# Weight sums staged in three tiles where rotation and decay tables lay, and GpSimd's order of sums and transfers written down

## Chip, cores and metric

One core of a Trainium2 chip. The metric is the device time of one execution in microseconds (us), the median of three runs. A profile of one further execution says what each engine did: TensorE (PE, its weight loads PEld), VectorE (DVE), ScalarE (ACT), GpSimd (POOL) and SyncE (SP), which here only issues transfers.

## What is computed

One inference step of a decoder layer over 1,088 tokens: a prompt of 1,024, and 8 sequences of 8 new tokens. All arrays are float32. Cut to what matters here:

```
h    = rmsnorm(x); proj = h @ w_in            # 1024 -> 4096 + 8 gates
ret  = retention(rotary(q), rotary(k), v)     # 4 heads of 128, in chunks of 128 tokens, decay tables
ml   = mlstm(q, k, v, gates)                  # 4 heads of 128, in chunks of 128 tokens
x    = x + rmsnorm(concat(ret, ml) @ w_out)
up   = rmsnorm(x) @ w_up                      # 1024 -> 2 * 2816 (gate and value)
act  = gelu(conv3(up)[gate]) * conv3(up)[value]
y    = x + rmsnorm(act @ w_down)
```

## The kernel before

A matrix product in float32 precision is made of three products of rounded halves: each operand is split into a high half (ACT, line 145) and a rest (DVE, line 147), and PE does high by high, high by rest and rest by high (lines 159 to 161 for the first two projections, 964 to 966 for the up-projection). The 1,088 tokens are four blocks of 272 columns.

Stages, in order of time: the retention heads with their projections (`mix_head(hd, False)`), the mLSTM heads (`mix_head(hd, True)`), the last gate projections with `mix_split`, the output projection (`out_proj`), the up-projection with convolution and gelu (one tile of 128 gate and 128 value columns per step, 22 steps, j = 0 to 21), and the down-projection.

The up-projection of tiles 2 to 21 uses a Strassen scheme of seven products in place of eight. It needs four sums of the four blocks A11, A12, A22 and A21 of each weight tile. They do not depend on the tokens, so they are made long before: `weight_sums` (line 689) runs on GpSimd while PE works on the mLSTM heads. For each of 40 parts (20 tiles, two halves of 256 columns each) it

- fetches the four blocks from `in_wu` in two transfers of 256 KB (line 698, issued on GpSimd's queue) into a tile of 128 x 1024,
- makes four sums in place, each 128 x 256 (line 710), the first three in a chain, where each reads the one before,
- stores the tile with one transfer of 512 KB to a DRAM scratch `sd` (line 711, GpSimd's queue too).

The up-projection later loads the sums from `sd` (line 904, two transfers of 256 KB for each pair of sums).

There are two tiles for the parts. They lie where the rotation tables `rot0` and `rot1` were, so the first fetch waits until the last retention head has rotated its keys (lines 440 and 441). The fetch of a part writes a tile whose earlier store has to land first. The retention's other tables (decay masks, `C_RM`, `C_RMS`; factors `C_ZE`, `C_XI`, `C_XI2`) and the identity are one tile `cst`; their last reader is the last retention head's `finish` (lines 593 and 596).

The order of instructions on an engine is set by a scheduler from estimated times, unless the program fixes it with `tc.issue_after(x)`: what is issued in that context comes behind x. All instructions of one engine run in that order, and one that waits holds up those behind it.

All tiles of the mixing stages lie in pools that are closed by `mixctx.close()` (line 745); the pool `fp`, which has the accumulators `oacc` of the output projection (line 791), tiles for its weights and the loads `xr` (line 816), is laid over their memory. A first write to such a tile waits for everything that still used the memory under it, the sums' tiles and their stores included. The output projection takes its weight tiles m = 0 to 7 through two staging tiles `st_out` (SP, line 133), and its first weight tiles are not in `fp`.

Of the kernel before, what the change touches and what calls it, by code (L numbers as in the profile page):

```python
# [10 lines left out]
F32 = mybir.dt.float32  # L11
# [3 lines left out]
ALU = mybir.AluOpType  # L15

P = 128
D = 1024
# [4 lines left out]
TS = NB * LS  # L23
T = LP + TS
# [12 lines left out]
HB = 2 * Q  # L37
# [7 lines left out]

C_ID, C_RM, C_RMS = 0, 128, 128 + 512
C_ZE, C_XI, C_XI2, C_BLK = C_RMS + 256, C_RMS + 264, C_RMS + 300, C_RMS + 336
C_N = C_BLK + 8
X_NEG, X_NEGS, X_SEL = 0, 128, 192
# [43 lines left out]
def hybrid_layer_kernel(ctx: ExitStack, tc: tile.TileContext, a: dict, o: dict):  # L93
    nc = tc.nc
# [125 lines left out]
    mp = mpool("mp", bufs=1)  # L220
    cst = mp.tile([P, C_N], F32, name="cst")
    rb = mp.tile([P, T], F32, name="rb")
# [9 lines left out]
    xs = [flat("x", b, k=KT) for b in range(4)]  # L232
    rot = [mp.tile([P, T], F32, tag=f"rot{i}", name=f"rot{i}") for i in range(2)]
    nc.sync.dma_start(vec, a["vec"])
    first = (2 * NH, 2 * NH + 1)
    staged = [stage_w(a["wi"][first[0]], f"in{first[0]}")]
    for b in range(4):
# [5 lines left out]
        if b == 1:  # L243
            for i in range(2):
                nc.sync.dma_start(rot[i], a["rot"][:, i * T:(i + 1) * T])
    nc.sync.dma_start(cst, a["cst"])
    nts = []
# [229 lines left out]
    def mix_head(hd, ml):  # L477
# [38 lines left out]
        def front(cs):  # L516
# [8 lines left out]
            if ml:  # L525
                nc.vector.tensor_tensor(kz[:n, :L], px[:n, 0, :L, :],
                                        cols[:n, c0:c0 + L, NH + hd].unsqueeze(2).broadcast_to([n, L, P]), ALU.mult)
            else:
                zc = C_ZE + hd + (0 if c0 < 8 else NH)
                nc.vector.tensor_scalar(kz[:n, :L], px[:n, 0, :L, :], cst[:n, zc:zc + 1], None, ALU.mult)  # L530
            vt = vts[0]
# [26 lines left out]
            else:  # L558
                m = cst[:, C_RM + hd * P:C_RM + (hd + 1) * P] if c0 < 8 else \
                    cst[:TS, C_RMS + hd * TS:C_RMS + (hd + 1) * TS]  # L560
                mk = m.unsqueeze(1).broadcast_to([n, L, n])
# [14 lines left out]
        def finish(on, mv, c0, L, name):  # L576
# [13 lines left out]
            else:  # L590
                xs_ = lambda t: cst[:n, t + 9 * hd + c0:t + 9 * hd + c0 + L]
                rd = xs_(C_XI)
# [96 lines left out]
    def weight_sums():  # L689
# [4 lines left out]

        def fetch(j, c):
            g = mp.tile([P, T], F32, tag=f"rot{c}", name=f"sg{j}_{c}")[:, :D]
            for q in range(2):
                nc.gpsimd.dma_start(g[:, q * 512:(q + 1) * 512].rearrange("p (b n) -> p b n", b=2),  # L698
                                    a["wu"][j, q].rearrange("p (b n) -> p b n", b=2)[:, :, cols(c)])
            held.append(g.rearrange("p (b n) -> p b n", b=4))  # L700

        fetch(*parts[0])
        for i, (j, c) in enumerate(parts):
            if i + 1 < len(parts):
                fetch(*parts[i + 1])
            g = held.pop(0)
            a11, a12, a22, a21 = (g[:, i, :] for i in range(4))
            for o_, x, y, op in ((a21, a11, a21, ALU.subtract), (a22, a22, a21, ALU.subtract),
                                 (a11, a22, a11, ALU.add), (a12, a12, a22, ALU.subtract)):
                nc.gpsimd.tensor_tensor(o_, x, y, op)  # L710
            nc.gpsimd.dma_start(sd[j][:, :, cols(c)], g)
            if c:
                yield
# [166 lines left out]
    def weight_prep(j):  # L880
# [19 lines left out]
        yield ws  # L900
        for i, names in ((1, ("S2", "S1")), (2, ("S4", "S3"))):
            st = wp.tile([P, 2 * HB], F32, tag="wst", name=f"st_up{j}_{i}")[:, :D]
            for c, name in enumerate(names):
                nc.sync.dma_start(st[:, c * D // 2:(c + 1) * D // 2], sd[j][:, ("S1", "S4", "S2", "S3").index(name), :])
            parts(i, st, *names)
            yield
# [431 lines left out]
```

## Time and profile before

| what | value |
|---|---|
| median of three runs | 1419.82 us (1418.65 to 1426.08) |
| the profiled execution: its own time | 1415.93 us |
| its span, from the first to the last instruction | 1414.1 us |
| granted TensorE clock, mean | 0.984 of full speed |
| busy: PE, PEld | 1346.1 us, 1320.2 us |
| busy: DVE, ACT, POOL | 1026.0 us, 587.9 us, 474.1 us |
| DMA: mean rate | 136 GB/s |

The profile page gives busy time by engine, then the span in 40 slices (35.4 us each), then groups of instructions by line. In such a group `out<-in` are names of the program, `x160` is a count, then come the busy time, the mean time of one in ns, and the idle time of the engine just before them with what ended it. "A <- B: total, times, longest" says that A waited for B. The chain that ended last is followed back from the last instruction. In a timeline a row is: start, duration, engine, line, operation, and in brackets the engine's idle time before it and what ended that.

### The profile page before, as it was taken

The numbers are of one execution on the slowest core, as the hardware profiler recorded it, in microseconds if no ns is written. First come the engines' busy times: TensorE is split into PE (matmuls) and PEld (weight loads), VectorE is DVE, ScalarE is ACT, GpSimd is POOL, SyncE is SP. The second block draws the span as 40 slices with busy tenths as digits, with TensorE's granted clock in tenths as the row PEclk, the third lists the DMA queues.
The fourth block names the chain that finished last, engine by engine and source line by source line (L and its number), as shares of the span: only waits on it lengthen the run. The fifth ranks groups of instructions, "written<-read, shape, count | busy, mean of one in ns | idle before, by whom it ended". The sixth has DMA issues, their size and how long they took to land.

```text
span 1414.1 us, 26967 instructions
## 1 busy us (share of the span) xinstructions
PE 1346.1 (95%) x10545; PEld 1320.2 (93%) x10545; DVE 1026.0 (73%) x2023; ACT 587.9 (42%) x1102; POOL 474.1 (34%) x605
## 2 busy tenths in 40 slices
PE   7999899999999998299999999999999999999995
PEld 7899899999999988299999999999999999999995
DVE  7845974566465477156889987877877888996677
ACT  6423542313223234144556444433433445454563
POOL 5200000366556667400243422122222126782000
PEclk9999999999999999699999999999999999999998
DMA  6112111366666655532314444344444359543363
GB/s 235 60 46 70 51 53 60 120 198 168 177 173 164 198 149 167 191 124 64 124 47 140 148 156 128 116 138 145 138 138 130 114 166 321 187 123 94 94 214 127
DMA packets 98494, 192.80 MB, mean 136 GB/s; under 512 B 16832, under 2 KB 41536, under 8 KB 97856
## 3 DMA queue, kind: packets, MB, share of 16 engines
q1 hardware_dynamic: 86208, 149.14, 32.8%
q0 software_dynamic: 12160, 41.95, 10.2%
q8 instruction: 83, 1.36, 0.4%
q14 instruction: 43, 0.35, 0.1%
HBM read 134.58 MB, written 56.47 MB: 135 GB/s over the span
## 4 chain that ended last, share of the span: by engine, by line
PE 65%; DMA 15%; POOL 8%; DVE 7%; issue 3%; ACT 2%; DVEq 0%; SPq 0%; POOLq 0%; ACTq 0%
DMA sg<-in_wu 8%; POOL sg L710 6%; DMA sd<-sg 6%; PE up_S L966 6%; PE up_S L965 6%; PE up_S L964 6%; PE dn L1161 4%; PE dn L1163 4%; PE dn L1162 4%; PE up_A L965 4%; PE up_A L964 4%; PE up_A L966 4%; PE in L161 4%; PE in L159 4%; PE in L160 4%
## 5 line engine op out<-in xcount | busy, mean ns | idle before, releaser
L159 PE MATMUL in<-hh,wh_in 128*128 128x272 f32 x1024 | 302.7, 296 | 12.2 <-ACT hh L199 6.8
L161 PE MATMUL in<-hh,wl_in 128*128 128x272 f32 x1024 | 300.4, 294 | 1.9 <-DVE wl_in L147 1.9
L160 PE MATMUL in<-hl,wh_in 128*128 128x272 f32 x1024 | 299.1, 292 | 1.2 <-DVE hl L200 1.2
L159 PEld LDWEIGHTS in<-hh,wh_in 128*128 128x128 f32 x1024 | 194.6, 190 | 14.9 <-ACT hh L199 6.8
L160 PEld LDWEIGHTS in<-hl,wh_in 128*128 128x128 f32 x1024 | 194.6, 190 | 3.9 <-issue 2.1
L161 PEld LDWEIGHTS in<-hh,wl_in 128*128 128x128 f32 x1024 | 193.9, 190 | 3.3 <-DVE wl_in L147 2.3
L145 ACT ACTIVATE wh_up<-st_up 128x1024 fp32r<-128x1024 f32 x84 | 80.5, 958 | 160.2 <-PE up_S L965 96.4
L710 POOL TENSOR_TENSOR sg<-sg 128x256 f32<-128x256 f32 x160 | 125.9, 815 | 58.0 <-DMA sg<-in_wu 55.6
L147 DVE TENSOR_TENSOR wl_up<-st_up,wh_up 128x1024 fp32r<-128x1024 f32 x84 | 96.8, 1153 | 7.9 <-ACT wh_up L145 7.8
L1090 DVE TENSOR_TENSOR rb<-rb 128x544 fp32r<-128x544 f32 x78 | 73.7, 950 | 34.6 <-ACT rb L1089 34.4
L938 DVE TENSOR_TENSOR Uv<-Uv,up_S 128x272 f32<-128x272 f32 (+1 forms) x200 | 66.6, 376 | 44.2 <-PE up_S L966 44.2
L994 POOL TENSOR_TENSOR act<-act 128x544 f32<-128x544 f32 x44 | 71.5, 1624 | 80.4 <-DMA bd<-act 57.4
L698 POOL DMA_DIRECT2D sg<-in_wu x80 | 57.2, 721 | 80.4 <-DMA sd<-sg 47.2
L1110 POOL TENSOR_TENSOR wd<-wd 128x512 f32<-128x512 f32 x44 | 75.7, 1747 | 23.6 <-DMA wd<-in_wd 12.5
L1089 ACT ACTIVATE rb<-rb 128x544 fp32r<-128x544 f32 x78 | 50.6, 651 | 75.4 <-DMA rb<-bd 63.1
L979 DVE SCALAR_TENSOR_TENSOR c<-Uv,vec,c 128x1024 f32<-128x1024 f32 (+1 forms) x88 | 70.5, 804 | 9.2 <-ACT c L977 9.2
L979 DVE SCALAR_TENSOR_TENSOR c<-Ug,vec,c 128x1024 f32<-128x1024 f32 x88 | 68.6, 818 | 1.9 <-ACT c L977 1.9
L159 PE MATMUL out<-mh,wh_out 128*128 128x272 f32 x128 | 39.2, 306 | 27.4 <-ACT wh_out L145 24.1
L977 ACT ACTIVATE c<-Ug,vec 128x1024 f32<-128x1024 f32 (+1 forms) x44 | 34.7, 835 | 54.9 <-DVE Ug L942 48.8
L145 ACT ACTIVATE wh_in<-st_in 128x1024 fp32r<-128x1024 f32 x32 | 33.9, 1058 | 50.5 <-PE in L160 46.9
L621 POOL TENSOR_TENSOR vx_r<-vts,cst 64x1024 f32<-64x1024 f32 x3 | 6.4, 2146 | 142.9 <-ACT vts L534 142.9
L159 PEld LDWEIGHTS out<-mh,wh_out 128*128 128x128 f32 x128 | 25.4, 199 | 28.2 <-issue 24.3
(541 smaller groups left out, 4661.0 us busy)
## 6 DMA issues: line engine op xcount, KB each, us to landing
rb<-bd SPq DMA_DIRECT2D x76, 272.0 KB, 2.9
sg<-in_wu POOLq DMA_DIRECT2D x80, 256.0 KB, 4.2
sd<-sg POOLq DMA_DIRECT2D x40, 512.0 KB, 3.6
st_up<-sd SPq DMA_DIRECT2D x80, 256.0 KB, 3.6
bd<-act SPq DMA_DIRECT2D x33, 544.0 KB, 4.9
st_in<-in_wi SPq DMA_DIRECT2D x32, 512.0 KB, 3.6
st_up<-in_wu SPq DMA_DIRECT2D x24, 512.0 KB, 3.4
wd<-in_wd SPq DMA_DIRECT2D x44, 256.0 KB, 4.4
```

The costliest lines, as they stand in the source:

```text
L145: nc.scalar.activation(hi, x, AF.Copy)
L147: eng.tensor_tensor(lo, x, hi.bitcast(F32), ALU.subtract)
L159: nc.tensor.matmul(ps, hi[:, ws], xh, start=k == 0, stop=False)
L160: nc.tensor.matmul(ps, hi[:, ws], xl, start=False, stop=False)
L161: nc.tensor.matmul(ps, lo[:, ws], xh, start=False, stop=k == KT - 1)
L710: nc.gpsimd.tensor_tensor(o_, x, y, op)
L964: nc.tensor.matmul(ps, wh[:, c], xh[:, k, n], start=k == 0, stop=False)
L965: nc.tensor.matmul(ps, wh[:, c], xl[:, k, n], start=False, stop=False)
L966: nc.tensor.matmul(ps, wl[:, c], xh[:, k, n], start=False, stop=k == 3)
L979: nc.vector.scalar_tensor_tensor(c, u(i), cw(i), c, ALU.mult, ALU.add)
L1090: nc.vector.tensor_tensor(lo, x, hi.bitcast(F32), ALU.subtract)
L1110: nc.gpsimd.tensor_tensor(quad(p, out), quad(p, x), quad(p, y), op)
```

## The change

- The constants are put in another order, and are split: `cst` keeps the identity and the block pattern (136 columns). A new tile `tab` of 3 x 1024 columns holds both rotation tables in its first 2 x 1088 columns and the other retention tables behind them.
- The parts of the weight sums use three slots of 1024 columns of `tab` in turn. Part i + 2 is fetched behind the sums and the store of part i, where before part i + 1 was fetched ahead of the sums of part i.
- Slot 0 lies over columns of the first rotation table, slot 1 over the rest of it and most of the second, slot 2 over the end of the second and the retention's other tables.
- `queued` writes GpSimd's order down: each fetch, sum and store of `weight_sums` comes behind the one before it in the program.
- The blocks in a slot are ordered A11, A22, A12, A21 (before A11, A12, A22, A21), so `sd` holds S1, S2, S4, S3, and the up-projection loads each pair of sums with one transfer of 512 KB.

```
-        def fetch(j, c):
-            g = mp.tile([P, T], F32, tag=f"rot{c}", name=f"sg{j}_{c}")[:, :D]
-            for q in range(2):
-                nc.gpsimd.dma_start(g[:, q * 512:(q + 1) * 512].rearrange("p (b n) -> p b n", b=2),
-                                    a["wu"][j, q].rearrange("p (b n) -> p b n", b=2)[:, :, cols(c)])
-            held.append(g.rearrange("p (b n) -> p b n", b=4))
-
-        fetch(*parts[0])
+        def queued(f, *args):
+
+            with tc.issue_after(last["sums"].ins) if "sums" in last else nullcontext():
+                last["sums"] = f(*args)
+
+        def fetch(i):
+            if i < len(parts):
+                j, c = parts[i]
+                g = tab[:, i % 3 * D:(i % 3 + 1) * D].rearrange("p (b n) -> p b n", b=4)
+                for q in range(2):
+                    queued(nc.gpsimd.dma_start, g[:, q::2, :], a["wu"][j, q].rearrange("p (b n) -> p b n", b=2)[:, :, cols(c)])
+                held.append(g)
+
+        fetch(0)
+        fetch(1)
         for i, (j, c) in enumerate(parts):
-            if i + 1 < len(parts):
-                fetch(*parts[i + 1])
             g = held.pop(0)
-            a11, a12, a22, a21 = (g[:, i, :] for i in range(4))
+            a11, a22, a12, a21 = (g[:, i, :] for i in range(4))
             for o_, x, y, op in ((a21, a11, a21, ALU.subtract), (a22, a22, a21, ALU.subtract),
                                  (a11, a22, a11, ALU.add), (a12, a12, a22, ALU.subtract)):
-                nc.gpsimd.tensor_tensor(o_, x, y, op)
-            nc.gpsimd.dma_start(sd[j][:, :, cols(c)], g)
+                queued(nc.gpsimd.tensor_tensor, o_, x, y, op)
+            queued(nc.gpsimd.dma_start, sd[j][:, :, cols(c)], g)
+            fetch(i + 2)
...
-    cst = mp.tile([P, C_N], F32, name="cst")
+    cst = mp.tile([P, C_RM], F32, name="cst")
+    tab = mp.tile([P, 3 * D], F32, name="tab")
+    rc = lambda c, n, rows=P: tab[:rows, 2 * T + c - C_RM:2 * T + c - C_RM + n]
...
-    rot = [mp.tile([P, T], F32, tag=f"rot{i}", name=f"rot{i}") for i in range(2)]
+    rot = [tab[:, i * T:(i + 1) * T] for i in range(2)]
...
-    nc.sync.dma_start(cst, a["cst"])
+    nc.sync.dma_start(cst, a["cst"][:, :C_RM])
+    nc.sync.dma_start(rc(C_RM, C_N - C_RM), a["cst"][:, C_RM:])
...
-        for i, names in ((1, ("S2", "S1")), (2, ("S4", "S3"))):
-            st = wp.tile([P, 2 * HB], F32, tag="wst", name=f"st_up{j}_{i}")[:, :D]
-            for c, name in enumerate(names):
-                nc.sync.dma_start(st[:, c * D // 2:(c + 1) * D // 2], sd[j][:, ("S1", "S4", "S2", "S3").index(name), :])
-            parts(i, st, *names)
+        sums = sd[j].rearrange("p b n -> p (b n)")
+        for i, names in ((1, ("S1", "S2")), (2, ("S4", "S3"))):
+            parts(i, stage_w(sums[:, (i - 1) * D:i * D], f"up{j}_{i}"), *names)
```

Two places show how instructions move. The first is GpSimd's program at the start of the weight sums. `sg_0` and `sg_1` are the two tiles of before, and rows with `in_wu` are fetches, rows with `sd` stores; `DMASW` waits are for transfers of GpSimd's queue, `DVE` and `DMAHW` waits are for VectorE and for a transfer of SP's queue, `Pool` waits for a sum. Before:

```order
L710 TENSOR_TENSOR sg_0_3836<-sg_0_3836 128x256 [waits DMASW1_49,DMASW0_49]
L710 TENSOR_TENSOR sg_0_3836<-sg_0_3836 128x256 [waits Pool_49]
L710 TENSOR_TENSOR sg_1_3839<-sg_1_3839 128x256 [waits DMASW3_49,DMASW2_49]
L710 TENSOR_TENSOR sg_0_3836<-sg_0_3836 128x256 [waits Pool_49]
L710 TENSOR_TENSOR sg_0_3836<-sg_0_3836 128x256
L710 TENSOR_TENSOR sg_1_3839<-sg_1_3839 128x256 [waits Pool_49]
L711 DMA sd<-sg_0_3836 512x1x256 [waits Pool_49]
L710 TENSOR_TENSOR sg_1_3839<-sg_1_3839 128x256 [waits Pool_49]
L710 TENSOR_TENSOR sg_1_3839<-sg_1_3839 128x256
L711 DMA sd<-sg_1_3839 512x1x256 [waits Pool_49]
L698 DMA sg_0_3847<-in_wu 128x2x256 [waits DMASW4_49]
L698 DMA sg_0_3847<-in_wu 128x2x256
```

After, behind the fetches of parts 0 and 1, with everything in the tile `tab`:

```order
L700 TENSOR_TENSOR tab<-tab 128x256 [waits DMASW1_49,DMASW0_49]
L700 TENSOR_TENSOR tab<-tab 128x256 [waits Pool_49] x2
L700 TENSOR_TENSOR tab<-tab 128x256
L700 DMA sd<-tab 512x1x256 [waits Pool_49]
L700 DMA tab<-in_wu 128x2x256 [waits DMAHW6_49,DVE_49]
L700 DMA tab<-in_wu 128x2x256 [waits DVE_49]
L700 TENSOR_TENSOR tab<-tab 128x256 [waits DMASW3_49,DMASW2_49]
L700 TENSOR_TENSOR tab<-tab 128x256 [waits Pool_49] x2
L700 TENSOR_TENSOR tab<-tab 128x256
L700 DMA sd<-tab 512x1x256 [waits Pool_49]
L700 DMA tab<-in_wu 128x2x256 [waits DMASW4_49]
L700 DMA tab<-in_wu 128x2x256
```

Before, two parts are summed with their sums mixed, both are stored, and only then the next two fetches stand, each behind a store that was issued just ahead. After, each part is sums, store, fetch; the fetch of part 2 waits for VectorE (the retention's tables in slot 2), and from part 3 on a fetch waits for the store of one part earlier (`DMASW4` is the store of part 0).

The second place is ScalarE's program at the start of the output projection. `mo` and `oacc` rows read the product of a weight tile (`out_0`), `wh_out` and `woh` rows make the high half of a weight tile, m = 2, 3 (`wh_out`), 4 (`woh`). Before:

```order
L797 ACTIVATE mo_6871<-out_0_6888,vec 128x272 [waits DVE_49,PE_49]
L738 ACTIVATE mh_6783<-yT_804 128x2x272 [waits DVE_49]
L799 ACTIVATE oacc_6881<-out_0_6888 128x272 [waits DMASW5_49,DMASW6_49,DMASW4_49,DMASW7_49,DMASW3_49,DMAHW1_49,DMASW2_49,DMAHW3_49,DMASW1_49,DMAHW6_49,DMASW0_49,DMAHW7_49,Activation_49,Pool_49]
L145 ACTIVATE wh_out_6917<-st_out_6915 128x1024 [waits DMAHW3_49]
L145 ACTIVATE wh_out_6951<-st_out_6949 128x1024 [waits DMAHW4_49]
L797 ACTIVATE mo_6871<-out_0_6921,vec 128x272 [waits PE_49]
```

After:

```order
L805 ACTIVATE mo_6831<-out_0_6848,vec 128x272 [waits DVE_49,PE_49]
L746 ACTIVATE mh_6743<-yT_804 128x2x272 [waits DVE_49]
L805 ACTIVATE mo_6831<-out_0_6881,vec 128x272 [waits PE_49]
L807 ACTIVATE oacc_6841<-out_0_6848 128x272 [waits DMASW5_49,DMASW6_49,DMASW4_49,DMASW7_49,DMASW3_49,DMAHW0_49,DMASW2_49,DMAHW2_49,DMASW1_49,DMAHW4_49,DMASW0_49,DMAHW7_49,Activation_49,Pool_49]
L145 ACTIVATE wh_out_6877<-st_out_6875 128x1024 [waits DMAHW4_49]
L807 ACTIVATE oacc_6841<-out_0_6881 128x272
L145 ACTIVATE wh_out_6911<-st_out_6909 128x1024 [waits DMAHW5_49]
L145 ACTIVATE woh_6943<-st_out_6945 128x1024 [waits DMAHW2_49]
```

The `oacc` row waits for all transfers of GpSimd's queue in both, and the weight tiles m = 2 and 3 stand behind it. After, one `mo` row, which reads the product of m = 1, stands ahead of it, and one `oacc` row between the two weight tiles. TensorE's own order is the same but for three matmuls, and the rest of ScalarE's and VectorE's differs by single rows.

More of the change, by code (lines that the diff above doesn't have):

```diff
@@ L44 @@
 V_N = V_BG + 2
-C_ID, C_RM, C_RMS = 0, 128, 128 + 512
-C_ZE, C_XI, C_XI2, C_BLK = C_RMS + 256, C_RMS + 264, C_RMS + 300, C_RMS + 336
-C_N = C_BLK + 8
+C_ID, C_BLK, C_RM, C_RMS = 0, 128, 136, 136 + 512
+C_ZE, C_XI, C_XI2 = C_RMS + 256, C_RMS + 264, C_RMS + 300
+C_N = C_XI2 + 36
 X_NEG, X_NEGS, X_SEL = 0, 128, 192
@@ L529, in front @@
                 zc = C_ZE + hd + (0 if c0 < 8 else NH)
-                nc.vector.tensor_scalar(kz[:n, :L], px[:n, 0, :L, :], cst[:n, zc:zc + 1], None, ALU.mult)
+                nc.vector.tensor_scalar(kz[:n, :L], px[:n, 0, :L, :], rc(zc, 1, n), None, ALU.mult)
             vt = vts[0]
@@ L558, in front @@
             else:
-                m = cst[:, C_RM + hd * P:C_RM + (hd + 1) * P] if c0 < 8 else \
-                    cst[:TS, C_RMS + hd * TS:C_RMS + (hd + 1) * TS]
+                m = rc(C_RM + hd * P, P) if c0 < 8 else rc(C_RMS + hd * TS, TS, TS)
                 mk = m.unsqueeze(1).broadcast_to([n, L, n])
@@ L590, in finish @@
             else:
-                xs_ = lambda t: cst[:n, t + 9 * hd + c0:t + 9 * hd + c0 + L]
+                xs_ = lambda t: rc(t + 9 * hd + c0, L, n)
                 rd = xs_(C_XI)
```

## Prediction

> **What bounds the kernel now.** The page's first two parts, then TensorE's waits over the whole span:
>
> ```profile
> span 1414.1 us, 26967 instructions
> PE   7999899999999998299999999999999999999995
> ...
> PE out L159 <- ACT wh_out L145: 24.1, 1, 24.1
> PE in L159 <- ACT hh L199: 6.8, 1, 6.8
> PE in L159 <- DVE z L468: 3.4, 3, 1.5
> PE out L159 <- DVE z L468: 3.2, 1, 3.2
> ```
>
> PE is at 9 tenths nearly everywhere; the 2 is the one hole. Of the waits listed, one is large: 24.1 us, once, at the output projection, for the high half of a weight tile on ACT. The timeline around it says why ACT was late:
>
> ```profile
> 566.54 0.66 ACT L738 ACTIVATE mh<-yT 128x544 fp32r<-128x544 f32 x1 [1.54 <-DVE yT L471]
> 590.21 0.40 ACT L799 ACTIVATE oacc<-out 128x272 f32<-128x272 f32 x1 [23.01 <-DMA sd<-sg]
> 590.50 1.99 ACT L145 ACTIVATE wh_out<-st_out 128x1024 fp32r<-128x1024 f32 x2
> 567.27 0.29 PE L161 MATMUL out<-mh,wl_out 128*128 128x272 f32 x1
> 591.65 0.57 PE L159 MATMUL out<-mh,wh_out 128*128 128x272 f32 x1 [24.09 <-ACT wh_out L145]
> ```
>
> ACT's `oacc` row is the first write over the mixing stages' memory; it waits 23.01 us for the last store of the weight sums, and the two weight tiles PE needs stand behind it. So GpSimd's side job, not on any path for 300 us, ends last here. Its groups, its landings, its start and its last part:
>
> ```profile
> L710 POOL TENSOR_TENSOR sg<-sg 128x256 f32<-128x256 f32 x160 | 125.9, 815 | 58.0 <-DMA sg<-in_wu 55.6
> L698 POOL DMA_DIRECT2D sg<-in_wu x80 | 57.2, 721 | 80.4 <-DMA sd<-sg 47.2 <-DVE k_r L440 33.2
> DMA to landing us min/median/max: 3.1/4.1/10.5
> 264.12 3.03 POOL L698 DMA_DIRECT2D sg<-in_wu  x4 [33.24 <-DVE k_r L440]
> 578.61 1.44 POOL L698 DMA_DIRECT2D sg<-in_wu  x2 [0.41 <-DMA sd<-sg]
> 583.16 2.99 POOL L710 TENSOR_TENSOR sg<-sg 128x256 f32<-128x256 f32 x4 [3.12 <-DMA sg<-in_wu]
> 586.45 0.75 POOL L711 DMA_DIRECT2D sd<-sg  x1 [0.30 <-POOL sg L710]
> 586.45 3.35 DMA sd<-sg
> ```
>
> It runs from 264.1 to 589.8 (586.45 + 3.35): 8.14 us for each of 40 parts. Fetches and stores cost GpSimd 55.6 + 47.2 = 102.8 us of waiting, 2.6 us a part: two tiles cannot cover a fetch and a store that land in about 4.1 us each.
>
> **The sums' new length.** The last part of before stands alone, as every part does after, so its rows are the price of one: 583.16 to 586.45 for four sums and the gap to the store (3.29), 0.74 to issue the store, 1.44 to issue two fetches: 5.47 us. These four sums took 2.99 / 4 = 748 ns each, the mean of all is 815, since VectorE runs beside most: + 0.27. Waiting for transfers: a fetch now has one whole part (5.7 us) until its sums, a store about as much until its slot is fetched; a median landing of 4.1 is covered, one of 10.5 leaves 4.8 us open. I add 0.46 (an estimate: about one part in ten meets such a landing). That is 6.2 us a part; the ends are 5.5 (nothing but the row) and 8.1 (what it costs now).
>
> The start does not move, but a wait is added. Slot 2 lies over the retention's tables, and its fetch stands in GpSimd's queue behind part 0. The tables' last reader:
>
> ```profile
> L596 DVE TENSOR_TENSOR A_r<-A_r,cst x8: 145/163/164, 130.8 to 308.1; 128x4 f32<-128x4 f32 x8
> ```
>
> So GpSimd stands until 308.1 + 0.16. Queued behind are only the sums; nobody else waits for them then. With two fetch issues that is 309.7; 39 parts follow, the last two without a fetch (2 x 1.44 = 2.9), and the last store's landing runs 2.6 past its issue (3.35 - 0.75): 309.7 + 39 x 6.2 - 2.9 + 2.6 = 551. With 5.5 it is 524, with 8.1 it is 625. ACT comes to its `oacc` row at about 567, so up to 6.6 us a part the sums no longer hold it; at 7.2 they end where they do now.
>
> **What is late next.** After, ACT does one `mo` row for tile m = 1 first, whose product PE ends at 567.6 (567.27 + 0.29): 0.5, then `oacc` 0.4, the weight tile m = 2 about 1.0 (1.99 / 2), `oacc` 0.4, tile m = 3 1.0, to 570.9. PE's program has two matmuls of m = 3 ahead of the third of m = 2, so it flows from 570.9. Before it flowed from 592.94:
>
> ```profile
> 533.71 30.90 SPq L133 DMA_DIRECT2D st_out<-in_wo  x3
> st_out<-in_wo SPq DMA_DIRECT2D x8, 512.0 KB, 4.6
> 592.55 0.60 PE L159 MATMUL out<-mh,wh_out 128*128 128x272 f32 x1
> 592.94 0.43 PE L160 MATMUL out<-ml,wh_out 128*128 128x272 f32 x1
> 593.40 0.43 PE L159 MATMUL out<-mh,wh_out 128*128 128x272 f32 x1
> 593.62 0.43 PE L160 MATMUL out<-ml,wh_out 128*128 128x272 f32 x1
> 595.21 0.29 PE L161 MATMUL out<-mh,wl_out 128*128 128x272 f32 x1
> 597.73 0.29 PE L159 MATMUL out<-mh,wh_out 128*128 128x272 f32 x1
> 597.86 0.29 PE L160 MATMUL out<-ml,wh_out 128*128 128x272 f32 x1
> 592.89 5.69 DMA st_out<-in_wo
> 599.72 0.40 PE L159 MATMUL out<-mh,woh 128*128 128x272 f32 x1
> ```
>
> 592.94 - 570.9 = 22.0. The data of m = 3 are there: the last of the first three loads was issued by 564.6 (533.71 + 30.90) and lands 4.6 later, at 569.2, before ACT turns to it at 569.9. Tile m = 4 goes into the staging tile that m = 2 frees, at 592.89 before, and reached PE 6.8 us later (599.72). After, m = 2 is ready on ACT at 569.5, and VectorE makes its rest about 1.2 us behind that (591.65 to 592.89 before), so 570.7 + 6.8 = 577.5 against 599.72: 22.2. The two chains agree; I take 22.2.
>
> Two small terms come on top. The first matmuls behind the hole stand 0.22 us apart until 595.21, later ones 0.13: a lower clock, 10 matmuls by 0.1 = 1.0 us. Whether that comes back behind the hole of 3.3 us that is left (567.6 to 570.9), no row shows; it is worth 0 to 1.0, and I take 0, since tile m = 4 comes at 577.5 either way. The Trainium skill, "TensorE: Matmul & The Clock Gate", "What's actually happening", states that the clock halves after an idle window of about 3.4 us; the rows agree (0.22 against 0.13 behind 24 us), and by that rule 3.3 us leave it up, which by itself would make the time 1394.8. The other term: just ahead of the hole VectorE is late for PE (3.4 + 3.2 us, the `z` rows at the top) while GpSimd's sums run. They go on until 551 in the forecast, and are gone for the last 16 us. What that is worth shows in one operation with two inputs in SBUF, before the sums and during them:
>
> ```profile
> L147 DVE TENSOR_TENSOR wl_in<-st_in,wh_in 128x1024 fp32r<-128x1024 f32 x8 | 9.8, 1220 | 1.2 <-ACT wh_in L145 1.2
> ...
> L147 DVE TENSOR_TENSOR wl_in<-st_in,wh_in 128x1024 fp32r<-128x1024 f32 x11 | 14.9, 1356 | 2.8 <-ACT wh_in L145 2.1
> ...
> 561.54 2.72 DVE L147 TENSOR_TENSOR wl_out<-st_out,wh_out 128x1024 fp32r<-128x1024 f32 x1
> ```
>
> On average 136 ns more, but 1.5 us in the last row. The 3.2 wait ends at 559.8, after the sums would have ended: I take 1.8 us of the 6.6, between 0 and 6.6. Sum: 22.2 + 1.8 = 24.0.
>
> **Edits counted at nothing.** In the up-projection 40 loads of 512 KB replace 80 of 256 KB:
>
> ```profile
> st_up<-sd SPq DMA_DIRECT2D x80, 256.0 KB, 3.6
> st_up<-in_wu SPq DMA_DIRECT2D x24, 512.0 KB, 3.4
> 780.00:1210.00 430.00, 430.00 (x3431) 430.00 (x3430) 355.66 (x608) 187.78 (x253) 122.61 (x200) 1.00 0.48 156
> ```
>
> A load of 512 KB lands no later (3.4 against 3.6), and PE, busy 430 of 430 us, hides all of it; were the cover gone, 40 loads by 0.2 us is 8 us either way. The rows for the last edit, and for the rivals:
>
> ```profile
> 590.92 0.42 SPq L877 DMA_DIRECT2D cache<-in_cache  x1
> 309.00:440.00 131.00, 131.00 (x1043) 126.19 (x1042) 69.83 (x219) 35.63 (x101) 84.08 (x114) 1.00 0.64 182
> GB/s 235 60 46 70 51 53 60 120 198 168 177 173 164 198 149 167 191 124 64 124 47 140 148 156 128 116 138 145 138 138 130 114 166 321 187 123 94 94 214 127
> ```
>
> The constants come in two loads where one was: one more issue on SP at the start, some 0.4 us (the first row), covered by PE's work on the value projections; uncovered, it costs that.
>
> **Rivals.** *Landings set the pace, and the kernel gets slower.* A part moves 1.05 MB; at 6.2 us that is 169 GB/s against 129 at 8.14, so the stage of 309 to 440 goes from 182 to 222 GB/s, and the DMA share from 0.64 to about 0.78. If landings grow with it, the three slots bind: a slot's round is three parts long, and from 7.2 us a part (21.6 us a round, landings of some 17 us where two medians make 8.2) the sums end later than now. At 8.1, 625 - 589.8 = 35 us late: 1455 us. Against it: another slice moved 321 GB/s. For it: landings up to 10.5 already. Between 6.6 and 7.2 lies the milder form: the sums still hold ACT, the gain is 0 to 22, about 1407.
>
> *VectorE is crowded.* Sums take 3.3 us of each 8.14 now and of each 6.2 after, 0.40 and 0.53 of the time, so the 136 ns above become about 180. In 309 to 440 VectorE is busy 69.83 of 131 us and PE waits for nothing, so it hides; in the last heads, where `z` rows are late already, it may cost up to 8 us: 1404. The Trainium skill, "SBUF — State Buffer", "Who interferes with whom", goes further: an operation of VectorE with two inputs in SBUF and one of GpSimd that reads SBUF lock each other out for a whole instruction. The 136 ns and the 2.72 us row agree; by that rule denser sums cost VectorE more, on the path only where PE already waits.
>
> *The change doesn't do it*: another condition in `oacc`'s long list (SP's transfers, GpSimd, ACT) is met as late as the store. Then 1419.8. Against it: the row names the store, and ACT resumed 0.4 us after it landed.
>
> **The numbers.** The profiled execution took 1415.93 us, its span 1414.1; 24.0 less is 1391.9. The median of the runs, 1419.82, is 3.9 above that execution, so I forecast 1395.8. Its own range goes from 1391 (all of the 6.6) to 1398 (nothing but the 22.2). Chances: forecast 0.80, milder form 0.08, VectorE crowded 0.06, landings slower 0.04, no effect 0.02. The range reaches to 1388 (2.3 us below 1391 for the spread of three runs) and to 1404, the crowded case; it leaves out 0.14 and some of the tails. A measurement of this kernel tells about 0.5%, 7.1 us, from no change. Faster by more: 0.80 + 0.06 + most of the milder form, 0.91; within it 0.05; slower 0.04.
>
> **What would show it.** In the profile after: GpSimd idle for some 33 us behind part 0, ended by the retention's last factor row near 308; then about 6.2 us a part with almost no waits for transfers; the last store near 551; no PE wait over 4 us at the output projection, and no slice with a 2. Wrong would be: a store of the sums later than 567, a PE wait for a weight tile over 5 us, or waits of PE for VectorE between 310 and 550, where there are almost none now.

## The result, and the profile after

The median fell from 1420.12 us (1416.98 to 1426.08, six runs) to 1398.53 us (1397.98 to 1402.11, six runs): a ratio of 0.9846, 95% interval 0.9822 to 0.987. That is 21.6 us less; the forecast was 24.0 less, 1395.8. The profiled execution after took 1397.98 us, span 1396.0, against 1415.93 and 1414.1 before: 18.1 us of span.

After, the page's first two parts, its transfers by size, and TensorE's longest waits between 264 and 575 us:

```profile
span 1396.0 us, 26912 instructions
PE   7999899999999998699999999999999999999995
DMA packets 92878, 192.80 MB, mean 138 GB/s; under 512 B 16208, under 2 KB 41040, under 8 KB 92240
PE out L159 <- ACT wh_out L145: 11.1, 2, 10.7
PE out L159 <- ACT mh L746: 2.4, 1, 2.4
PE in L159 <- DVE A_m L598: 1.5, 1, 1.5
```

The hole is there still, less than half as long: 10.7 us where 24.1 stood, a 6 in place of the 2. Its releaser is the same. The timeline around it, ACT's rows, then PE's:

```profile
572.30 0.40 ACT L807 ACTIVATE oacc<-out 128x272 f32<-128x272 f32 x1 [8.59 <-DMA sd<-tab]
572.59 1.05 ACT L145 ACTIVATE wh_out<-st_out 128x1024 fp32r<-128x1024 f32 x1
555.22 0.36 PE L159 MATMUL out<-mh,wh_out 128*128 128x272 f32 x1 [2.42 <-ACT mh L746]
573.74 0.56 PE L159 MATMUL out<-mh,wh_out 128*128 128x272 f32 x1 [10.72 <-ACT wh_out L145]
579.85 0.35 PE L159 MATMUL out<-mh,wh_out 128*128 128x272 f32 x1
```

ACT still waits in front of `oacc` for the sums' last store, 8.59 us where it waited 23.01. The sums end sooner, not soon enough. GpSimd's side, in the timeline: the two waits for the tables, the second part's store, the last part's; and the last store in the chain of waits.

```profile
293.25 0.71 POOL L700 DMA_DIRECT2D tab<-in_wu  x1 [21.46 <-DVE pt_r L568]
306.43 0.72 POOL L700 DMA_DIRECT2D tab<-in_wu  x1 [12.46 <-DVE A_r L598]
310.52 0.75 POOL L700 DMA_DIRECT2D sd<-tab  x1 [0.30 <-POOL tab L700]
568.55 0.74 POOL L700 DMA_DIRECT2D sd<-tab  x1 [0.30 <-POOL tab L700]
568.55 3.33 DMA sd<-tab
```

The sums end at 568.55 + 3.33 = 571.9; before, they ended at 589.8. The difference, 17.9 us, is nearly the whole 18.1 us by which the two spans differ: PE's first matmul behind the hole moved from 591.65 to 573.74, also 17.9. From the second part's store at 310.52 to the last one's at 568.55 there are 38 parts, 6.79 us each. Where that is more than the 6.2 of the forecast shows in the groups of GpSimd's sums, in its waits from 306 to 575 us, and in the longest pieces of the chain of waits there:

```profile
L700 POOL TENSOR_TENSOR tab<-tab 128x256 f32<-128x256 f32 x160 | 131.9, 835 | 20.2 <-DMA tab<-in_wu 12.9
POOL tab L700 <- DMA sd<-tab: 22.7, 3, 9.7
POOL tab L700 <- DMA tab<-in_wu: 10.6, 3, 7.7
345.97 15.61 DMA sd<-tab
398.11 13.77 DMA tab<-in_wu
452.77 13.58 DMA tab<-in_wu
506.45 14.13 DMA sd<-tab
```

A sum takes 835 ns in the mean, against 815 before. And GpSimd does not wait a little in many parts: it waits long in few, 22.7 + 10.6 = 33.3 us in six waits, around four transfers that took 13.6 to 15.6 us. The four are some 53 us apart, one for each mLSTM head. SyncE's timeline has, just ahead of each:

```profile
344.16 0.67 SPq L639 DMA_DIRECT2D out_ns<-sb_m  x1
397.64 0.68 SPq L639 DMA_DIRECT2D out_ns<-sb_m  x1
451.50 0.67 SPq L639 DMA_DIRECT2D out_ns<-sb_m  x1
504.63 0.68 SPq L639 DMA_DIRECT2D out_ns<-sb_m  x1
```

Line 639 stores a head's normaliser state, 128 x 8 numbers, from a tile of 129 columns for each sequence, of which it takes the last: 1,024 single numbers, each 4 bytes and 516 from the next. Two stretches just behind such a store (busy time of POOL, then granted clock, DMA share, GB/s) show what happens to the transfers beside it; the last line is the whole stage, with PE, PEld, DVE, ACT and POOL ahead of the same three figures:

```profile
340.00:350.00 10.00, 9.05 (x14) 1.00 1.03 181
400.00:410.00 10.00, 3.90 (x6) 1.00 1.05 142
309.00:440.00 131.00, 131.00 (x1043) 126.18 (x1042) 71.98 (x219) 35.78 (x101) 103.41 (x135) 1.00 0.78 203
```

The DMA engines are fully busy there while they move 142 to 181 GB/s, though a slice of before moved 321. Over the whole stage the share is 0.78, the figure that the forecast worked out, but it had it for 222 GB/s, and here 203 were moved.

### The profile page after: what moved, and what is told of

Its sections match the earlier page's. It is cut to its first block, busy times and chain, and to the rows that moved or that the text cites. A ratio compares the mean times of both kernels' runs of the same rounds, so it can differ in the third digit from the quotient of the medians.

```text
span 1396.0 us, 26912 instructions
## 1 busy us (share of the span) xinstructions
PE 1346.0 (96%) x10545; PEld 1320.9 (95%) x10545; DVE 1025.8 (73%) x2023; ACT 587.9 (42%) x1102; POOL 476.9 (34%) x605
## 4 chain that ended last, share of the span: by engine, by line
PE 68%; POOL 12%; DVE 8%; DMA 6%; issue 5%; ACT 2%; DVEq 0%; SPq 0%; ACTq 0%; POOLq 0%
POOL tab L700 10%; PE up_S L972 6%; PE up_S L971 6%; PE up_S L970 6%; PE dn L1167 5%; PE dn L1169 5%; PE dn L1168 5%; PE up_A L971 4%; PE up_A L970 4%; PE up_A L972 4%; PE in L161 4%; PE in L159 4%; PE in L160 4%; DMA tab<-in_wu 2%; DMA sd<-tab 2%
## 5 line engine op out<-in xcount | busy, mean ns | idle before, releaser
L159 PE MATMUL in<-hh,wh_in 128*128 128x272 f32 x1024 | 303.0, 296 | 10.9 <-ACT hh L199 6.4
L700 POOL TENSOR_TENSOR tab<-tab 128x256 f32<-128x256 f32 x160 | 131.9, 835 | 20.2 <-DMA tab<-in_wu 12.9
L700 POOL DMA_DIRECT2D tab<-in_wu x80 | 56.8, 717 | 89.0 <-DVE k_r L443 32.4
L147 DVE TENSOR_TENSOR wl_in<-st_in,wh_in 128x1024 fp32r<-128x1024 f32 x32 | 40.7, 1272 | 10.6 <-ACT wh_in L145 9.8
```

The costliest lines, as they stand in the source:

```text
L147: eng.tensor_tensor(lo, x, hi.bitcast(F32), ALU.subtract)
L159: nc.tensor.matmul(ps, hi[:, ws], xh, start=k == 0, stop=False)
L700: last["sums"] = f(*args)
```

## The experiments

Four theories were put to the test, under these names in the expectations.

- **T1** (theory 1): the time follows the end of the sums, one to one, until ACT no longer waits in front of `oacc`; earlier ends bring nothing.
- **T3**: GpSimd's sums also cost time because VectorE is slower beside them.
- **A**: the four long landings, and so the 6.79 us a part, come from the scattered stores of line 639, not from the sums' own traffic.
- **L**: writing GpSimd's order down matters because it leaves VectorE gaps between a part's sums, not because it makes the sums shorter.

Theory 2 of the expectations (weight loads and ACT's order hold PE anyway) forecasts no change where the sums end sooner; `no_arith` and `small_tables` rule it out.

Their results in one table, with the issue of the sums' last store and PE's longest wait for `wh_out` from the profile of each. The ratio is to the kernel before, run on the same chip. The medians come from several chips, on which before took 1416.97 to 1420.12 us; so a few us between two rows count only where the gains over before on each row's own chip differ as well.

| kernel | last store issued | PE waits | median us | ratio, 95% interval |
|---|---|---|---|---|
| `two_slots` | 637.80 | 83.6 | 1467.75 | 1.0362 (1.0338 to 1.0386) |
| `before_merged` | 591.56 | 34.4 | 1422.49 | 1.0025 (1.0006 to 1.0044) |
| before | 586.45 | 24.1 | 1420.12 | |
| `before_ns` | 570.23 | 10.5 | 1400.89 | 0.9876 (0.9835 to 0.9917) |
| after | 568.55 | 10.7 | 1398.53 | 0.9846 (0.9822 to 0.987) |
| `free_order` | 560.05 | 0.4 | 1406.25 | 0.9908 (0.9875 to 0.9942) |
| `small_tables` | 551.22 | 0.7 | 1387.61 | 0.9803 (0.9774 to 0.9831) |
| `indep_sums` | 535.94 | 0.7 | 1392.43 | 0.9818 (0.9764 to 0.9873) |
| `ns_store` | 534.86 | 0.7 | 1387.45 | 0.9776 (0.9746 to 0.9807) |
| `ns_compact` | 532.37 | 0.7 | 1392.47 | 0.9825 (0.9796 to 0.9854) |
| `small_ns` | 524.14 | 0.7 | 1386.75 | 0.9767 (0.974 to 0.9795) |
| `no_arith` | 498.95 | 0.4 | 1382.64 | 0.9765 (0.974 to 0.9791) |

**`no_arith`** is after without the four sums of each part; the up-projection's sums are therefore not made, only moved.

```
-                queued(nc.gpsimd.tensor_tensor, o_, x, y, op)
```

> Leaves out the four sums of every part, so the stored blocks are the plain ones; fetches, stores and their order stay. In the changed kernel the sums end at 571.9 and PE waits 10.7 us for a weight tile behind them. Theory 1 (the end of the sums' last store is what holds TensorE, and nothing else of the sums costs anything): without the sums a part is some 4 to 5 us, the last store lands before 520, the wait of 10.7 falls to about 3.3, and the time is 7.4 us under the changed kernel: 1391. Theory 2 (the weight loads and ScalarE's order of the output projection hold PE anyway): no change, 1398. Theory 3 (VectorE, crowded by the sums, is a cost of its own): lower than 1389, since its late rows ahead of the output projection (2.4 + 1.5 + 0.9 us of PE waits) go as well.

1382.64 us (1381.4 to 1385.9): 8.4 below T1's number, within T3's. The hole is gone, as both say; TensorE's longest waits between 264 and 575 us:

```profile
PE out L159 <- DVE z L471: 1.4, 1, 1.4
PE out L161 <- DVE wol L147: 1.0, 2, 0.7
PE out L159 <- ACT woh L145: 0.9, 1, 0.9
PE out L159 <- ACT wh_out L145: 0.7, 2, 0.4
```

T1 missed in its estimate of what is left once the hole is gone, not in the hole: sums that end early enough, but are made, give 1386.75 (below). The 4.1 us between the two are no proof of T3: they come from two chips, before took 1419.45 us on one and 1417.27 on the other, and the two ratios, 0.9767 and 0.9765, are the same within their intervals.

**`two_slots`** is after with two slots in turn, the order as written.

```
-                g = tab[:, i % 3 * D:(i % 3 + 1) * D].rearrange("p (b n) -> p b n", b=4)
+                g = tab[:, i % 2 * D:(i % 2 + 1) * D].rearrange("p (b n) -> p b n", b=4)
```

> The changed kernel with two slots in turn in place of three (part i + 2 into the slot of part i), the order still written down: the fetch now waits for the store issued right ahead of it. Theory 1: a part is 3.4 of sums, 0.3, a store that has to land (4.2), two fetch issues 1.4: about 9.3 us, 40 parts from 267, and the long landings on top, so the sums end near 645, and the time follows one to one: 1398 + 73 = 1471, between 1455 and 1485. Rival (the written order is what brings the gain, the third slot little): within 5 us of 1398.

1467.75 us (1466.68 to 1468.38), 3.2 below the number. GpSimd's waits from 306 us on, and TensorE's longest:

```profile
POOL tab L700 <- DMA sd<-tab: 130.2, 34, 10.3
PE out L159 <- ACT wh_out L145: 84.0, 2, 83.6
```

With two slots the fetch written behind a store goes into that store's own tile and waits for it in nearly every part: 130.2 us in 34 waits. The third slot is what makes the written order pay; without it, it is 50.5 us slower than the kernel before (1417.27 on its chip).

**`small_tables`** is after with the three small factor tables (`C_ZE`, `C_XI`, `C_XI2`) in `cst`, so that slot 2's last readers end sooner.

```
-C_ID, C_BLK, C_RM, C_RMS = 0, 128, 136, 136 + 512
-C_ZE, C_XI, C_XI2 = C_RMS + 256, C_RMS + 264, C_RMS + 300
-C_N = C_XI2 + 36
+C_ID, C_BLK, C_ZE, C_XI, C_XI2 = 0, 128, 136, 144, 180
+C_RM, C_RMS = 216, 216 + 512
+C_N = C_RMS + 256
```

> The factors C_ZE, C_XI and C_XI2 (80 columns) go into the tile of the identity, so slot 2 lies over the end of the second rotation table and the decay masks alone. GpSimd's second wait for the tables then ends at about 293 (last read of the masks), not at 306.4: 13 us earlier. Theory 1: the sums end at 559, ahead of ScalarE's oacc row, and PE's wait of 10.7 falls to about 3.3: 7.4 us less, 1391. Theory 2 (weight loads hold PE anyway): 1398.

1387.61 us (1386.33 to 1392.03); its profiled execution was its slowest. The last store's issue moved to 551.22, and PE's wait for `wh_out` fell to 0.7 us:

```profile
551.22 0.74 POOL L700 DMA_DIRECT2D sd<-tab  x1 [0.30 <-POOL tab L700]
```

The issue is 17.3 us earlier than after, and the time 10.9 lower; as gains over before on each one's chip it is 29.7 against 21.6, 8.1 more. Either is about as much as the wait that was left (8.59 us of ACT, 10.7 of PE). T1 holds, its number was 3.4 us too high.

**`ns_compact`** is after with the normaliser state loaded and stored through a compact tile of 128 x 8, VectorE copying to and from it.

```
-            nc.sync.dma_start(sb[:, :, P], a["sn"][hd])
+            nst = m2.tile([P, NB], F32, tag="nst", bufs=1, name=f"nst_{nm}")
+            nc.sync.dma_start(nst, a["sn"][hd])
+            nc.vector.tensor_copy(sb[:, :, P], nst)
...
-                nc.sync.dma_start(o["ns"][hd], sb[:, :, P])
+                nso = m2.tile([P, NB], F32, tag="nst", bufs=1, name=f"nso_{nm}")
+                nc.vector.tensor_copy(nso, sb[:, :, P])
+                nc.sync.dma_start(o["ns"][hd], nso)
```

> The normaliser state of a head is loaded and stored through a tile of 8 columns (rows of 32 bytes), with one VectorE copy each way, in place of transfers that gather 1024 single values of 4 bytes. In the changed kernel the four landings of 13.6 to 15.6 us begin right behind the stores at the end of each head (344, 398, 451, 505), where the DMA share is 1.0 and the rate 100 to 200 GB/s, and GpSimd waits 33.3 us for them. Theory A (the single values of 4 bytes clog the DMA engines): these landings fall to about 5, GpSimd's waits for transfers to under 8, the sums end near 545, and PE's hole to about 3.3: 1391 or a little less. Theory B (it is the 512 KB state stores and loads beside them): the landings stay above 10, the sums end near 570, and the time stays at 1398.

1392.47 us (1389.93 to 1393.44), 1.5 above the number: the sums' last store was issued at 532.37, but the time stood 5 us above `ns_store` (below), which has the store alone, and 7 by the gains over before on each one's chip. The copy behind the load cost what the sums gave. VectorE's waits, then TensorE's:

```profile
DVE sb_m L518 <- DMA nst_m<-in_sn: 11.8, 3, 5.7
PE o_m L666 <- DVE S_m L672: 3.3, 3, 2.1
PE in L159 <- DVE q_m L434: 3.1, 2, 2.9
```

VectorE stood 11.8 us for a load, and PE waited for what was queued behind the copy.

**`ns_store`** keeps only the store half of that edit (the last three + lines).

> The changed kernel with only the normaliser state's store made compact; its load still gathers single values. ns_compact lost some 6 us because VectorE's copy behind the load stood 11.8 us waiting for it, with TensorE's o_m and q_m waits behind. Theory A (the scattered store is what clogs the DMA engines): the landings of 13.6 to 15.6 us go to under 8, the sums end before 550, and without the waiting copy the time is 1386 to 1389. Rival (the scattered load clogs as much): two or three landings above 10 stay, the sums end at 555 to 565, and the time is 1389 to 1394.

1387.45 us (1385.87 to 1389.9). Theory A holds; the load of the same single numbers (line 516) and the 512 KB state transfers of theory B are still there. The same page rows as above, then GpSimd's waits from 306 to 575 us, and the two stretches:

```profile
DMA packets 89295, 192.81 MB, mean 139 GB/s; under 512 B 12624, under 2 KB 37456, under 8 KB 88656
POOL tab L702 <- DMA sd<-tab: 0.9, 1, 0.9
POOL tab L702 <- DMA tab<-in_wu: 0.3, 1, 0.3
340.00:350.00 10.00, 9.13 (x13) 1.00 0.73 230
400.00:410.00 10.00, 9.35 (x14) 1.00 0.97 284
534.86 0.74 POOL L702 DMA_DIRECT2D sd<-tab  x1 [0.30 <-POOL tab L702]
```

The bytes are the same, the packets under 512 B fewer by 3,584: four stores of 1,024 single numbers less four of 128 rows. With that the waits of GpSimd fell from 33.3 us to 1.2, and the two stretches moved 230 and 284 GB/s where 181 and 142 went. So the long landings did not come from the sums' own traffic. The Trainium skill, "DMA: Bandwidth & Descriptors", "Rules for kernel authors", says that a transfer whose last dimension is not contiguous becomes one descriptor for each element; the count of packets here agrees.

**`small_ns`** joins `small_tables` and `ns_store`.

> small_tables with the normaliser state stored through a tile of 8 columns (the load stays as it was). Its sums should end near 525, 40 us ahead of the output projection, where in small_tables alone they end at about 555, ten us ahead. Theory 1 (only the end of the sums counts, once it is early enough nothing more is won): the same as small_tables, 1387.6, within 2. Theory 3 (VectorE, crowded by the sums in the last gate projections, costs PE some 5 us, the difference between small_tables and the run without the sums): those waits of PE for VectorE (3.7 + 2.0 + 1.3 in small_tables) go, and the time is 1383 to 1385.

1386.75 us (1384.16 to 1388.2), the fastest of the kernels that still make the sums. The sums' last store was issued 10.7 us before that of `ns_store`, and the time is the same within the runs' spread: T1's flat end, nearer to T1 than to T3.

**`before_ns`** makes `ns_store`'s edit in the kernel before.

> The kernel before with only the normaliser state's store made compact (rows of 32 bytes through a tile of 8 columns). Its four long landings (10.5, 7.7, 9.6 and 8.5 us) should go to about 4.5 and with them some 20 us of GpSimd's waits; a part is still fetched behind a store just issued. Theory 1 with theory A: the sums end at about 570 in place of 589.8, and the time falls one to one, to 1398 to 1403, about as much as the whole change brought. Rival (before, the landings were not what set the pace): within 4 us of before.

1400.89 us (1400.15 to 1402.39), against 1416.97 for before on the same chip. The sums end at 573.6, and ACT's row says the rest:

```profile
573.98 0.40 ACT L801 ACTIVATE oacc<-out 128x272 f32<-128x272 f32 x1 [11.19 <-DMA sd<-sg]
```

So three lines in the old order bring 16.1 us, three quarters of the whole change's 21.6. Both together bring 32.0 (1419.45 less 1387.45), less than the sum of 37.7, because the path stops following the sums once they end before ACT's row.

**`free_order`** is after with the three slots, and without the written order.

```
-            with tc.issue_after(last["sums"].ins) if "sums" in last else nullcontext():
-                last["sums"] = f(*args)
+            f(*args)
```

> The changed kernel with three slots and the loads of the sums as they are, but the order of GpSimd's sums and transfers left to the scheduler, which puts two parts' sums together, both stores behind them and two fetches behind those, as before the change. Theory 1: the third slot does not help where a fetch still stands behind a store just issued; a part costs 7.5 to 8.5 us, the sums end between 590 and 640 since GpSimd also waits for the tables, and the time is 1416 to 1465. Rival (the third slot alone brings the gain): the sums end near 572, 1398.

1406.25 us (1399.74 to 1411.43), between the two numbers and a miss for the first. The sums ended sooner than after (last store issued at 560.05), and PE lost the time elsewhere. TensorE's waits, then a place in VectorE's and GpSimd's timelines:

```profile
PE in L159 <- DVE q_m L434: 13.1, 3, 5.4
PE yt_m L603 <- DVE on_m L601: 5.3, 2, 2.8
396.62 4.14 POOL L699 TENSOR_TENSOR tab<-tab 128x256 f32<-128x256 f32 x6
397.41 3.59 DVE L596 TENSOR_SCALAR vv_m<-vv_m 128x4 f32<-128x4 f32 x1
```

PE waits 13.1 + 5.3 = 18.4 us for VectorE in the mLSTM heads, where after has 1.5. In the rows, GpSimd makes six sums without a gap, until 400.76; an operation of VectorE on 128 x 4 numbers, begun beneath them, ends at 401.00. So the written order is worth some 8 us, though the sums end later with it. This made theory L.

**`indep_sums`** is after with four operations that each read one block alone, so that no sum waits for the one before and the gaps go; the sums are then not the reference's.

```
-            for o_, x, y, op in ((a21, a11, a21, ALU.subtract), (a22, a22, a21, ALU.subtract),
-                                 (a11, a22, a11, ALU.add), (a12, a12, a22, ALU.subtract)):
+            for o_, x, y, op in ((a21, a21, a21, ALU.subtract), (a22, a22, a22, ALU.subtract),
+                                 (a11, a11, a11, ALU.add), (a12, a12, a12, ALU.subtract)):
```

> The changed kernel with four operations of each part that do not read one another (each block with itself), so the results are not the sums of the reference; count, sizes and order stay, but the waits of 0.07 us between chained sums are gone. In free_order, where sums of two parts stand interleaved and six run without a gap, VectorE's operations of 128 x 4 took 0.50 us in the mean of the mLSTM heads and up to 3.6 us (0.27 in the changed kernel, 0.15 without sums), and PE waited 18 us for VectorE there. Theory L (VectorE gets in between two operations of GpSimd only where GpSimd has a gap, so the chain's gaps keep it going): the mean of these small operations rises to 0.35 or more, PE's waits for VectorE between 264 and 500 us rise from 0 to 3 us or more, and the time to 1400 or more in spite of a part that is 0.2 us shorter. Rival (runs of six or more are needed, four are harmless): means and waits as in the changed kernel, the sums end up to 8 us earlier, the time is 1391 to 1398.

1392.43 us (1388.98 to 1396.99): the rival's number, not theory L's, though not for the rival's reason. The operations were shorter than expected (a median of 607 ns; 738 after), and the last store came 32.6 us sooner than after, not 8. The time stays some 5 us above that of `ns_store`, whose last store came as early; in the two profiles all of that lies in the down projection, 255.2 us from its first `ra_whi` matmul to the end against 250.2, for which no run shows a cause. Single rows do show L's mechanism, a VectorE operation that ends with a run of four gapless sums (393.08 + 2.32 = 395.40):

```profile
393.08 2.32 POOL L700 TENSOR_TENSOR tab<-tab 128x256 f32<-128x256 f32 x4
393.15 2.27 DVE L590 TENSOR_TENSOR vv_m<-mv_m,rd_m 128x4 f32<-128x4 f32 x1
```

But PE's waits for VectorE from 264 to 500 us are 0.2 us in all, so a block of 2.3 us does not reach PE. Nor do longer ones explain `free_order` by themselves: the kernel before also makes runs of six sums, and has no such waits of PE. Theory L in its form (the gaps) falls; what remains is that in `free_order` small operations of VectorE were hit more often and for longer (their mean from 264 to 500 us, over forms of 128 x 4 and 64 x 1, is 498 ns; 265 after, 208 before). Before has eleven runs of five or six sums in that time, and none of these operations took over 1.2 us there. Why the runs fell on them in `free_order` is open.

**`before_merged`** is before with the new block order in `sd` and one load of 512 KB for each pair of sums in the up-projection.

> The kernel before with one part of the change: the blocks of a part ordered A11, A22, A12, A21 and the sums loaded with one transfer of 512 KB for two. All theories: the same as before within 0.3% (TensorE is busy all of the up-projection); a gain over 4 us would mean that the merged loads had a share in the result.

1422.49 us (1418.48 to 1426.62, ten runs), the same as expected: ratio 1.0025 (1.0006 to 1.0044). The merged loads bring nothing and cost at most some 6 us; in its profile the last store also came 5.1 us later, at 591.56, which by T1 alone would account for its small loss.

## Why the prediction was right, and where it was not

The time came out near the forecast, but two of the signs of being wrong that the forecast had named came too: a store of the sums later than 567 (568.55), and a PE wait for a weight tile over 5 us (10.72). Its main case, sums that no longer hold ACT, did not happen.

**Right: the bound and the path.** The sums' last store held ACT's `oacc`, and PE behind it. The kernels put in order of that store (the table) give times that fall with it about one to one down to where ACT stops waiting, and hardly any more from there. Three stand outside: `free_order` and `ns_compact`, by VectorE's waits, and `indep_sums`, by its down projection.

**Right: the wait for the tables.** Forecast: GpSimd stands until 308.3. It stood until 306.43, in two waits of 21.46 and 12.46 us, because the two halves of part 2's fetch lie over different tables. Nobody waited for it meanwhile, but `small_tables` shows its price of some 8 to 11 us, since the sums were still the bound.

**The step that failed: "That is 6.2 us a part", and so "the last store's landing ... = 551".** It was 6.79 and 571.9. Of its three terms, the 5.47 from the last part's rows held. VectorE's part was 4 x (835 - 748) = 0.35 in place of 0.27. The landings' part was 33.3 / 38 = 0.88 in place of 0.46. Together 6.70; 0.09 is left over, of which two idle stretches of GpSimd without a releaser in the profile make 0.07 (2.6 us). Without the scattered stores a part takes (534.86 - 310.96) / 38 = 5.89 us, which is 5.47, 4 x (824 - 748) = 0.30 for VectorE, and almost nothing for landings (310.96 is the second part's store there):

```profile
310.96 0.75 POOL L702 DMA_DIRECT2D sd<-tab  x1 [0.30 <-POOL tab L702]
```

The forecast took the longest landing of before, 10.5 us, which leaves 4.8 us open, and put it on one part in ten. How often was right: it is 4 parts of 40. What it cost was wrong: 33.3 / 4 = 8.3 us each time. The four were in the trace of before, one per head, in the chain of waits:

```profile
347.65 10.53 DMA sd<-sg
400.56 7.66 DMA sd<-sg
452.90 9.60 DMA sg<-in_wu
507.63 8.49 DMA sd<-sg
```

Had these four been looked up beside SyncE's rows, their source would have been known. That they would grow to 13.6 to 15.6 us no row of before shows; that denser traffic around them made them grow is argued, and no run isolates it.

**The rival that came.** Landings did set the pace, in the milder form, 6.6 to 7.2 us a part, with the sums still holding ACT. Its price of about 1407 was the middle of a wide band. The forecast's own line gives 309.7 + 39 x 6.79 - 2.9 + 2.6 = 574.2, 15.6 us ahead of 589.8; GpSimd was released 1.9 us sooner than forecast, which makes 17.5, and 17.9 was measured.

**Why the total is near all the same.** The sums ended 20.9 us later than forecast, but the forecast had some 16 us of slack between them and ACT's `oacc` row, so only the rest could hold ACT up: it waited 8.59 us. PE, on the other hand, reached the output projection 4.6 us sooner (next paragraph). From these rows 22.2 + 4.6 - 8.6 = 18.2, and the span fell by 18.1. By the medians the whole gain is 21.6, by the profiled pair 18.0 (1415.93 less 1397.98): the profiled execution stood 4.2 us below its median before and 0.6 after. So the forecast is 2.7 us off by medians and 6.0 by the profiled pair. The second is the fair measure of the step; that the first is so small is luck.

**The 1.8 us of late `z` rows.** PE began the output projection at 555.22; before, that wait ended at 559.8, 4.6 us later. That is more than the 1.8 taken, inside the 0 to 6.6 that was given; 0.9 of it was there before any sum was made (VectorE's last rotation of keys began at 262.5, before at 263.4). It brought nothing after, since the hole's end was set by the sums; it only made ACT's wait for them longer. Where the sums were out of the way it counted: PE began at 556.16 in `ns_store`, 3.6 us sooner than before, and the span is 27.9 us shorter, against 22.2 + 3.6 = 25.8; 2.1 are left over.

**The clock behind the hole.** Behind it two dozen matmuls stand 0.22 us apart, until 579.85, and 0.13 from there on: some 2.2 us, where before lost 1.0. The granted clock is 0.50 from 574.2 to 579.8, and 1.00 from 580.2 on. The forecast took 0, and said that no row shows what a hole of 3.3 us does to the clock. A row of before comes near: PE waited 3.16 us ahead of its matmul at 559.76, and from 561.1 to 564.4 the granted clock is 0.50. After has the same behind the wait of 2.42 us at 555.22, which stands in the timeline at the top; the clock is 0.50 from 556.3 to 559.5:

```profile
556.24 0.43 PE L160 MATMUL out<-ml,wh_out 128*128 128x272 f32 x1
556.46 0.43 PE L161 MATMUL out<-mh,wl_out 128*128 128x272 f32 x1
```

The Trainium skill, "TensorE: Matmul & The Clock Gate", "What's actually happening", has the clock halved after an idle window of about 3.4 us. The 10.7 us of after fit that; the waits of 2.42 and 3.16 us do not. Nor does the length of a wait decide by itself: behind 2.00 us `small_ns` has the clock at 0.50 from 563.5 to 566.8, and behind the same 2.0 us `ns_store` has its matmuls 0.13 apart at once (565.97, 566.10, 566.23). What decides is open.

**Nothing, as forecast:** the merged loads (`before_merged`). The split constants have no run of their own. **VectorE crowded** did not come after (PE busy 236.00 of 236.00 us from 264 to 500), and came in `free_order`. The Trainium skill, "SBUF — State Buffer", "Who interferes with whom", was weighed as the rule against the change: an operation of VectorE and one of GpSimd lock each other out for one instruction. The rows fit a lock, and show more than one instruction: 2.27 and 3.59 us under runs of four and six sums.

**Open:** whether the sums cost anything beside their end (T3). The two ratios of `small_ns` and `no_arith` do not tell it, and in the two profiles, whose spans are 5.0 us apart, little of the difference can be the sums': 1.4 us are there before the first sum (GpSimd's first fetch at 260.24 and 258.88), 0.6 come until the output projection (553.47 and 551.51), 0.3 until the down projection's first `ra_whi` matmul (1133.0 and 1130.7), and 2.7 behind that, long after the sums. From that matmul to the end the profiles of all the kernels take 249.1 to 255.2 us, whenever their sums end, so single profiles do not resolve less than some 5 us. T1's flat end is no finer: `small_ns` is 3.0 us ahead of `ns_store` at that matmul, and loses 2.1 behind it.

## What to carry to other kernels

When a transfer now and then takes three times its median, put the long ones in order of time before giving them a mean: if they come once per iteration of some loop, look for what that loop stores beside them, and count its packets rather than its bytes. A job off to the side is worth shortening only until the row that waits for it stops waiting; read that slack first (here 23 us), and expect two cures for the same job to bring less than their sum (here 32.0 us for 37.7). A copy that makes a transfer compact belongs on the side where nobody waits: ahead of the store no wait for it showed, behind the load it held VectorE's queue for 11.8 us.

## What was not expected of the hardware

- A store of 4 KB as 1,024 pieces of 4 bytes, issued in 0.67 us, took the DMA engines' share to 1.03 to 1.05 at 142 to 181 GB/s, and transfers of 256 and 512 KB beside it landed in 13.6 to 15.6 us (median of the sums' transfers otherwise 4 to 5). Beside the same 4 KB as 128 rows no transfer of the sums took over 7.5 us.
- A VectorE operation on 128 x 4 numbers can last until a whole run of GpSimd's sums is over, not one of them: 3.59 us under six, 2.27 under four; under the runs of six in the kernel before none did.
- Four operations of GpSimd that each read one block alone took 2.32 us, four with two blocks each and three in a chain 2.99 to 3.06 in quiet parts. The chain is the small part of that: a sum that reads the one before begins about 0.08 us after its end (268.42 to 268.50 after), and the median of one is 737 or 738 ns in chains (after) and mixed (`free_order`), 607 with one block.
